# A 512-byte-per-partition copy as the first DMA on the ScalarE queue of a pooling kernel

## The chip, the core and the metric

The kernel runs on one core of a Trainium2 chip. Times are device microseconds (us); the time of a kernel is the median over its runs. Kernel before: 393.96 us, median of 3 runs (393.93 to 393.99). The core has compute engines with queues of their own (here VectorE and ScalarE do the arithmetic), SyncE, which here only issues DMAs, and 16 DMA engines that move data between the chip's memory (HBM) and the core's SBUF, which has 128 partitions. In the profile DVE is VectorE, ACT is ScalarE, SP is SyncE, and ACTq and SPq are the instruction queues from which ScalarE and SyncE issue DMAs.

## The reference

The kernel computes power-average pooling over windows of four along the last axis, with p = 2. `x` has 32 x 256 x 4096 float32 values, the result 32 x 256 x 1024.

```python
for i in range(out_length):                      # out_length = length // 4
    window = np.abs(x[:, :, 4*i:4*i + 4]) ** p    # p = 2
    result[:, :, i] = (np.mean(window, axis=-1)) ** (1.0 / p)
```

Each output is the square root of a quarter of the sum of four squares. 134.2 MB are read and 33.6 MB written, each once.

## The kernel before

The input is seen as one flat stream, cut into 20 loads of 128 rows, one row for each partition. A row has 13184 values (52,736 bytes, 6592 KB for the 128); load 3 has 13152 and load 19 has 11680. Loads are grouped into six blocks whose rows are contiguous in HBM: four of four loads, then loads 18, 16, 17, then load 19. One store writes the results of one block, so there are six stores.

Three tiles `xt` take the loads in turn. For each load i: ScalarE squares the tile in place (`square`, line 89), VectorE adds neighbours in two steps (`pairs`, line 95, then `fours`, line 99, to a quarter of the width), ScalarE takes the root with a scale of one quarter (`root`, line 102). The sums and roots of blocks 0 to 3 lie in `ot`, one slot for each load of the block; sums of loads 4, 8, 12 and 16 go first to PSUM (`st`), so that they need not wait for the store of the block before. The results of the last two blocks lie in the freed columns of an `xt` tile.

The order of the instructions on each engine is written out by hand (`tc.manual_schedule()`): each engine runs its own in program order, and semaphores make it wait for others.

- SyncE issues all 20 loads (line 83): three before the loop, then load i + 3 as soon as `fours` of load i is done, since it overwrites the same tile. It also issues the stores of blocks 3, 4 and 5 (line 86). These DMAs are queue q1.
- ScalarE issues the stores of blocks 0, 1 and 2 (line 86, called by `roots` for loads 3, 7 and 11), right after the block's last root. These are queue q10. The first is issued when load 3's results are ready.
- Before its first square ScalarE runs a root on a one-column tile `first`; the load of its function table stands ahead of it.
- VectorE's first instruction of its own is `pairs` of load 0.

For loads 18 and 19 VectorE squares part of the columns itself (line 155).

Of the kernel before, what the change touches and what calls it, by code (L numbers as in the profile page):

```python
# [1 line left out]

# [4 lines left out]


@with_exitstack
def kernel(  # L10
    ctx: ExitStack,
    tc: tile.TileContext,
    x: bass.AP,
    p: float,
    kernel_size: int,
    out: bass.AP,
):

    nc = tc.nc

    assert float(p) == 2.0, "kernel specialized for p == 2"
    k = int(kernel_size)  # L30
    assert k == 4, "kernel specialized for kernel_size == 4"

    P = nc.NUM_PARTITIONS
    fp32 = mybir.dt.float32
    Act = mybir.ActivationFunctionType
    add = mybir.AluOpType.add
    xf = x.rearrange("b c l -> (b c l)")
    of = out.rearrange("b c l -> (b c l)")
    total = xf.shape[0] // P

    W = 13184
    R = W // k
    X_SLOTS = 3
    NARROW = W - 32
    LAST = total - 18 * W - NARROW
    widths = [W] * 3 + [NARROW] + [W] * 15 + [LAST]
    n = len(widths)
    assert 0 < LAST <= W and LAST % 16 == 0


    blocks = [[0, 1, 2, 3], [4, 5, 6, 7], [8, 9, 10, 11], [12, 13, 14, 15], [18, 16, 17], [19]]
    block_of = {i: b for b, group in enumerate(blocks) for i in group}
    block_width = [sum(widths[i] for i in group) for group in blocks]

    x_pool = ctx.enter_context(tc.tile_pool(name="x_pool", bufs=1))
    o_pool = ctx.enter_context(tc.tile_pool(name="o_pool", bufs=1))
    s_pool = ctx.enter_context(tc.tile_pool(name="s_pool", bufs=1, space=bass.MemoryType.PSUM))
    x_tiles = [x_pool.tile([P, W], fp32, name=f"xt{j}") for j in range(X_SLOTS)]
    o_tile = o_pool.tile([P, 4 * R], fp32, name="ot")
    first = o_pool.tile([P, 1], fp32, name="first")  # L60
    s_tile = s_pool.tile([P, 4096], fp32, name="st")
    ctx.enter_context(tc.manual_schedule())

    def rows(flat, b, div):
        at = sum(block_width[:b]) * P // div
        return flat[at:at + block_width[b] * P // div].rearrange("(p w) -> p w", p=P)


    free = x_tiles[17 % X_SLOTS]
    place = {i: o_tile[:, i % 4 * R:i % 4 * R + widths[i] // k] for i in range(16)}  # L70
    place[18] = free[:, R:2 * R]
    place[19] = free[:, 0:LAST // k]
    place[16] = free[:, 2 * R:3 * R]
    place[17] = free[:, 3 * R:4 * R]
    held = [o_tile[:, 0:w // k] for w in block_width[:4]] + [free[:, R:4 * R], place[19]]

    xs, loads, stores, sums, squares = {}, {}, {}, {}, {}

    def load(i):
        b = block_of[i]  # L80
        at = sum(widths[j] for j in blocks[b][:blocks[b].index(i)])
        xs[i] = x_tiles[i % X_SLOTS][:, 0:widths[i]]
        loads[i] = nc.sync.dma_start(out=xs[i], in_=rows(xf, b, 1)[:, at:at + widths[i]])  # L83

    def store(b, queue):
        stores[b] = queue.dma_start(out=rows(of, b, k), in_=held[b])  # L86

    def square(v):
        return nc.scalar.activation(out=v, in_=v, func=Act.Square)  # L89

    def pairs(v):

        q = v.rearrange("p (n j) -> p n j", j=k)
        h = v[:, 0:v.shape[1] // 2].rearrange("p (n j) -> p n j", j=2)
        return nc.vector.tensor_tensor(out=h, in0=q[:, :, 0:2], in1=q[:, :, 2:4], op=add)  # L95

    def fours(o, v):
        h = v[:, 0:v.shape[1] // 2].rearrange("p (n j) -> p n j", j=2)
        return nc.vector.tensor_tensor(out=o, in0=h[:, :, 0], in1=h[:, :, 1], op=add)  # L99

    def root(o, s):
        return nc.scalar.activation(out=o, in_=s, func=Act.Sqrt, scale=1.0 / k)  # L102

    summed = {i: s_tile[:, 0:R] if i in (4, 8, 12, 16) else place[i] for i in range(n)}

    def roots(*group):
        if len(group) == 1:
            root(place[group[0]], summed[group[0]])
        else:
            v = o_tile[:, group[0] % 4 * R:(group[-1] % 4 + 1) * R]  # L110
            r = root(v, v)
            if group[0] in (5, 9):

                implied(r, stores[block_of[group[0]] - 1])
        if group[-1] in (3, 7, 11):
            store(block_of[group[-1]], nc.scalar)

    def implied(later, earlier):

        tc.declare_no_dep(later.ins, earlier.ins, reason="implied by the other waits")  # L120

    for i in range(X_SLOTS):
        load(i)


    ahead = {4: (3,), 8: (7,), 12: (11,)}
    behind = {3: [(0, 1, 2)], 7: [(5, 6), (4,)], 11: [(9, 10), (8,)], 14: [(12,)], 15: [(13, 14)], 16: [(15,)]}

    root(first[:, :], nc.const_aps.tensor(1.0, (P, 1), fp32))
    for i in range(17):  # L130
        if i in ahead:
            roots(*ahead[i])
        s = square(xs[i])
        squares[i] = s
        if i == 3:
            implied(s, squares[0])
        if i in (3, 7, 11):

            for earlier in sums[i - X_SLOTS]:
                implied(s, earlier)  # L140
        for group in behind.get(i, []):
            roots(*group)
        sums[i] = pairs(xs[i]), fours(summed[i], xs[i])
        if i + X_SLOTS < n:
            load(i + X_SLOTS)

    store(3, nc.sync)
    square(xs[17])
    pairs(xs[17])
    fours(summed[17], xs[17])  # L150
    later = {18: 4608, 19: 2000}

    def shared_square(i):
        v = xs[i][:, 0:later[i]]
        nc.vector.tensor_tensor(out=v, in0=v, in1=v, op=mybir.AluOpType.mult)  # L155
        square(xs[i][:, later[i]:widths[i]])

    def shared_pairs(i):
        implied(pairs(xs[i]), loads[i])

    shared_square(18)
    roots(16)
    roots(17)
    shared_pairs(18)
    fours(summed[18], xs[18])
    shared_square(19)
    roots(18)
    store(4, nc.sync)
    shared_pairs(19)
    fours(summed[19], xs[19])  # L170
    roots(19)
    store(5, nc.sync)


# [1 line left out]
_INS = ['x', 'p', 'kernel_size']  # L176
_OUTS = [((32, 256, 1024), 'float32')]

_NUMBERS = {'p': 2.0, 'kernel_size': 4}


# [26 lines left out]
```

## Time and profile before

| What | Value |
|---|---|
| time, median of 3 runs | 393.96 us (393.93 to 393.99) |
| span of the profiled execution, first to last instruction | 392.3 us |
| time of the runs outside such a span | 1.7 us (393.96 - 392.3) |
| ACT busy | 274.4 us (70%), 37 instructions |
| DVE busy | 218.2 us (56%), 42 instructions |
| DMA moved | 167.77 MB, mean 428 GB/s, 3744 packets |
| chain that ended last | DMA 43%, ACT 30%, DVE 23% |

The profile lists no time of its own for the profiled execution beside its span; the runs' times are those of the table. A line of the timeline has start, duration, engine, source line, operation and its tiles, and in brackets how long the engine was idle before it and what ended that. A line of a table by stretches has the stretch, its length, busy time and number of instructions of DVE, ACT and POOL, TensorE's clock, the mean busy share of the DMA engines and GB/s; a DMA packet is counted whole in the stretch in which it starts, so a short stretch can have a share above 1. A line of the DMA issues has tiles, issuing queue, number, KB each and the median us from issue to landing; a line of the DMA queues has packets, MB and the share of the 16 engines' span.

The 3744 packets are 26 DMAs of 128 rows and 16 semaphore writes each: one packet for a row, and 8 rows on each of the 16 engines.

### The profile page before, as it was taken

To read this page: it belongs to the slowest core of one execution; us is meant where nothing else is said; L and a number is where in the kernel's file an instruction comes from. 1 tells how busy PE (TensorE), PEld (TensorE's weight loads), DVE (VectorE), ACT (ScalarE), POOL (GpSimd) and SP (SyncE) were. 2 spreads that over 40 slices of the span, in tenths; PEclk is the share of its full clock that TensorE was granted. 3 is DMA by queue.
4 is the path that set the end of the run, shared out by engine and by line. 5 is a ranking of instruction groups with operands and counts; after the bars stand their busy time and mean duration, and the time that the engine had idled before them with its cause. 6 is when DMAs were issued, how large, how long until landed. Compare 5 with 4: busy or idle time off the path is not lost.

```text
span 392.3 us, 176 instructions
## 1 busy us (share of the span) xinstructions
DVE 218.2 (56%) x42; ACT 274.4 (70%) x37; POOL 0.2 (0%) x4
## 2 busy tenths in 40 slices
DVE  0009477580693274905942748069418485699970
ACT  1095695979950859799509597995098999969910
POOL 0000000000000000000000000000000000000000
DMA  8999999999999999999999999999999999999997
GB/s 344 430 430 430 430 440 435 452 457 366 430 430 430 430 430 430 430 441 446 452 446 441 436 430 436 430 430 430 430 430 430 430 430 430 430 453 415 430 413 342
DMA packets 3744, 167.77 MB, mean 428 GB/s; under 512 B 416, under 2 KB 416, under 8 KB 416
## 3 DMA queue, kind: packets, MB, share of 16 engines
q1 hardware_dynamic: 3312, 147.53, 87.4%
q10 hardware_dynamic: 432, 20.25, 11.9%
HBM read 134.22 MB, written 33.55 MB: 428 GB/s over the span
## 4 chain that ended last, share of the span: by engine, by line
DMA 43%; ACT 30%; DVE 23%; issue 0%; ACTq 0%; SPq 0%; DVEq 0%
DMA xt<-in_x_dram 43%; ACT xt L89 28%; DVE xt L95 14%; DVE ot L99 5%; DVE xt L99 3%; DVE xt L155 2%; ACT ot L102 2%; ACT xt L102 1%; ACTq L86 0%; SPq L83 0%; DVEq L95 0%
## 5 line engine op out<-in xcount | busy, mean ns | idle before, releaser
L89 ACT ACTIVATE xt<-xt 128x13184 f32<-128x13184 f32 (+3 forms) x20 | 216.7, 10847 | 92.3 <-DMA xt<-in_x_dram 91.0
L95 DVE TENSOR_TENSOR xt<-xt 128x6592 f32<-128x6592 f32 (+2 forms) x20 | 139.7, 6985 | 144.1 <-ACT xt L89 143.9
L99 DVE TENSOR_TENSOR ot<-xt 128x3296 f32<-128x3296 f32 (+1 forms) x13 | 46.7, 3592 | 17.9 <-DMA out_dram<-ot 17.6
L102 ACT ACTIVATE ot<-ot 128x6592 f32<-128x6592 f32 (+3 forms) x8 | 37.2, 4655 | 7.0 <-DVE ot L99 7.0
L102 ACT ACTIVATE xt<-xt 128x3296 f32<-128x3296 f32 (+1 forms) x3 | 8.5, 2836 | 8.8 <-DVE xt L99 8.8
L99 DVE TENSOR_TENSOR st<-xt 128x3296 f32<-128x3296 f32 x4 | 14.4, 3600 | 0.1
L99 DVE TENSOR_TENSOR xt<-xt 128x3296 f32<-128x3296 f32 (+1 forms) x3 | 10.4, 3461 | 0.1
L102 ACT ACTIVATE ot<-st 128x3296 f32<-128x3296 f32 x3 | 8.7, 2898 | 0.0
L155 DVE TENSOR_TENSOR xt<-xt 128x4608 f32<-128x4608 f32 (+1 forms) x2 | 7.2, 3593 | 0.0
L102 ACT ACTIVATE xt<-st 128x3296 f32<-128x3296 f32 x1 | 2.9, 2898 | 0.0
L102 ACT ACT_TABLE_LOAD x1 | 1.3, 1283 | 0.7 <-PEq L189 0.7
L102 ACT ACTIVATE first<-const-float32-1.0 128x1 f32<-128x1 f32 x1 | 0.2, 202 | 0.0
L189 POOL MEMSET const-bfloat16-1.0<- 128x1 bf16 x1 | 0.1, 101 | 0.0
L189 POOL MEMSET const-uint8-127<- 128x1 uint8 x1 | 0.1, 101 | 0.0
L189 POOL MEMSET const-float32-0.0<- 128x1 f32 x1 | 0.1, 98 | 0.2 <-issue 0.2
L189 POOL MEMSET const-float32-1.0<- 128x1 f32 x1 | 0.1, 98 | 0.0
## 6 DMA issues: line engine op xcount, KB each, us to landing
xt<-in_x_dram SPq DMA_DIRECT2D x18, 6592.0 KB, 29.8
out_dram<-ot ACTq DMA_DIRECT2D x2, 6592.0 KB, 35.1
out_dram<-ot SPq DMA_DIRECT2D x1, 6592.0 KB, 37.1
out_dram<-ot ACTq DMA_DIRECT2D x1, 6588.0 KB, 36.3
xt<-in_x_dram SPq DMA_DIRECT2D x1, 6576.0 KB, 24.7
xt<-in_x_dram SPq DMA_DIRECT2D x1, 5840.0 KB, 21.9
out_dram<-xt SPq DMA_DIRECT2D x1, 4944.0 KB, 16.1
out_dram<-xt SPq DMA_DIRECT2D x1, 1460.0 KB, 8.2
```

The lines of the kernel that those rows point to most:

```text
L89: return nc.scalar.activation(out=v, in_=v, func=Act.Square)
L95: return nc.vector.tensor_tensor(out=h, in0=q[:, :, 0:2], in1=q[:, :, 2:4], op=add)
L99: return nc.vector.tensor_tensor(out=o, in0=h[:, :, 0], in1=h[:, :, 1], op=add)
L102: return nc.scalar.activation(out=o, in_=s, func=Act.Sqrt, scale=1.0 / k)
L155: nc.vector.tensor_tensor(out=v, in0=v, in1=v, op=mybir.AluOpType.mult)
L189: nc = _bacc.Bacc("TRN2", target_bir_lowering=False, num_devices=1)
```

## The change

Two tiles of 128 columns, `zeros` and `spare`, are added in SBUF, behind the tiles that are there. Ahead of everything else VectorE sets `zeros` to 0. After the first three loads (which SyncE issues), ScalarE issues a DMA that copies `zeros` to `spare`, 512 bytes on each of 128 partitions, 64 KB in all. In ScalarE's program it stands ahead of the one-column root. It waits for the memset. Nothing reads `spare`.

```diff
     o_tile = o_pool.tile([P, 4 * R], fp32, name="ot")
     first = o_pool.tile([P, 1], fp32, name="first")
     s_tile = s_pool.tile([P, 4096], fp32, name="st")
+    zeros = o_pool.tile([P, 128], fp32, name="zeros")
+    spare = o_pool.tile([P, 128], fp32, name="spare")
     ctx.enter_context(tc.manual_schedule())
...
+    nc.vector.memset(zeros[:, :], 0.0)
     for i in range(X_SLOTS):
         load(i)
+    nc.scalar.dma_start(out=spare[:, :], in_=zeros[:, :])
```

## The prediction

> **What bounds the kernel now.** I read the page first: its slices, its DMA queues and its issues.
>
> ```profile
> DMA  8999999999999999999999999999999999999997
> q1 hardware_dynamic: 3312, 147.53, 87.4%
> q10 hardware_dynamic: 432, 20.25, 11.9%
> out_dram<-ot SPq DMA_DIRECT2D x1, 6592.0 KB, 37.1
> out_dram<-xt SPq DMA_DIRECT2D x1, 4944.0 KB, 16.1
> out_dram<-xt SPq DMA_DIRECT2D x1, 1460.0 KB, 8.2
> ```
>
> The 16 DMA engines work in every slice; the two queues' shares add to 99.3% of the span. q1 is SyncE's queue (20 loads, the last three stores), q10 ScalarE's (the first three stores). That this holds to the last microsecond is seen from the last stores: they are issued at 339.1, 371.8 and 383.1 us and land at 376.2, 387.9 and 391.3, so 4944 KB took 11.7 us and 1460 KB took 3.4, the rate of the loads (6592 KB in 15.57 us, 423 KB/us). ScalarE (70%) and VectorE (56%) wait. So time taken from the DMA engines' stream comes off the span, and time added to it goes on.
>
> Then the timeline, for the first square on each load's landing and the issues between.
>
> ```profile
> 0.73 1.28 ACT L102 ACT_TABLE_LOAD   x1 [0.73 <-PEq L189]
> 0.73 1.33 SPq L83 DMA_DIRECT2D xt<-in_x_dram  x3
> 2.02 0.20 ACT L102 ACTIVATE first<-const-float32-1.0 128x1 f32<-128x1 f32 x1
> 18.79 11.19 ACT L89 ACTIVATE xt<-xt 128x13184 f32<-128x13184 f32 x1 [16.56 <-DMA xt<-in_x_dram]
> ...
> 65.47 11.16 ACT L89 ACTIVATE xt<-xt 128x13152 f32<-128x13152 f32 x1 [4.34 <-DMA xt<-in_x_dram]
> ...
> 90.31 0.38 ACTq L86 DMA_DIRECT2D out_dram<-ot  x1
> ...
> 144.41 11.19 ACT L89 ACTIVATE xt<-xt 128x13184 f32<-128x13184 f32 x1 [4.36 <-DMA xt<-in_x_dram]
> ...
> 222.22 11.19 ACT L89 ACTIVATE xt<-xt 128x13184 f32<-128x13184 f32 x1 [4.38 <-DMA xt<-in_x_dram]
> ...
> 300.07 11.19 ACT L89 ACTIVATE xt<-xt 128x13184 f32<-128x13184 f32 x1 [1.58 <-DMA xt<-in_x_dram]
> ```
>
> Between these landings the engines move four loads and one store each time. 144.41 to 222.22 is 77.81 us, 222.22 to 300.07 is 77.85; 65.47 to 144.41, with the same bytes but 4 KB, is 78.94. So about 1.1 us are lost once, in the stretch that holds the first DMA on q10 (issued at 90.31). To find the place I asked for short stretches in which each of the 16 engines starts one row of a load or store. A packet is counted whole in the stretch where it starts, so the DMA share (the sixth number) times the width is the mean time of one packet.
>
> ```profile
> 1.70:2.60 0.90, 0.00 (x0) 0.51 (x2) 0.00 (x0) 1.00 2.96 938
> 4.30:4.90 0.60, 0.00 (x0) 0.00 (x0) 0.00 (x0) 1.00 3.25 1406
> 89.80:90.40 0.60, 0.00 (x0) 0.47 (x1) 0.00 (x0) 1.00 3.29 1406
> 91.80:92.40 0.60, 0.00 (x0) 0.60 (x1) 0.00 (x0) 1.00 4.82 1406
> 94.70:95.50 0.80, 0.00 (x0) 0.80 (x1) 0.00 (x0) 1.00 2.45 1054
> 170.55:171.30 0.75, 0.00 (x0) 0.75 (x1) 0.00 (x0) 1.00 2.60 1125
> 248.35:249.05 0.70, 0.00 (x0) 0.70 (x1) 0.00 (x0) 1.00 2.79 1205
> ```
>
> A row takes 1.95 us (4.30: 3.25 x 0.60). The rows started at 91.8 take 4.82 x 0.60 = 2.89 us, 0.94 more, on all engines at once; rows 1.3 us behind the second and third store's issues take 1.95. In the packet records those slow rows are still loads; the first store row starts at 94.8, after them. The only other slow rows are the very first, at 1.7 us: 2.96 x 0.90 = 2.66, 0.72 more. So both queues show one stall of 0.7 to 1.1 us, at their first DMA. SyncE's first store, at 339, shows none.
>
> **The change, part by part.** It removes nothing. It adds a memset of 128x128 f32 on VectorE, one DMA issue on ScalarE, and 64 KB of SBUF to SBUF traffic on q10, so that store 0 is no longer q10's first DMA.
>
> Memset: VectorE's adds take 7.03 us for 6592 columns, 1.07 ns each, so 0.14 us, up to 0.2 with the 0.1 us of a one-column memset as its fixed part. VectorE's first work comes at 30.01: free. Issue: 0.34 to 0.38 us on ScalarE (the three stores' rows), behind a wait for the memset, at about 0.95 if nothing is ahead of it. Queued behind it are the table load (1.28) and the one-column root (0.20), which then end near 2.9 instead of 2.2; the next, the square at 18.79, waits for load 0: free. SyncE's loads wait for none of this. No wait is added later, since nobody reads the spare tile, and the big tiles stay where they are.
>
> The copy's traffic: 128 rows over 16 engines, 8 packets of 512 B and a semaphore write each. By bytes alone 64 KB at 423 KB/us is 0.15 us. The packet records have 11,680 B at 0.438 us and 52,736 B at 1.947: a line through both gives 9 ns a packet and 0.037 ns a byte, 0.028 us for 512 B, so 8 x 0.028 = 0.22 us on each engine. I take 0.22, nearest in kind; ends 0.15 and 0.4 (double, for small packets that nothing here shows). It lies in a full stream, so it counts.
>
> The Trainium skill, in DMA: Bandwidth & Descriptors, section Bandwidth, measures 0.95 us for a lone 64 KB load and calls such transfers dominated by descriptors; by that the sum would be 0.73 us worse, about no change. I keep the row, since here the packets stand between those of loads.
>
> The stall at 91.8: it goes if it belongs to the queue's first DMA: -1.10 us by the landings (ends 0.94 by the rows, 1.13 by the longest difference). What replaces it at the start is not in the trace. Below, 0: the engines start the first rows at 1.74 to 2.49 and are slow there anyway; q10's first packets, issued 0.22 us after q1's, would arrive from 1.96 on, while those rows still wait (they end at 4.35 to 4.8, so data flow from 2.40 to 2.85). Above, 1.1, the whole stall in series. The nearest row is q1's own start, whose wait covers q10's arrival on most engines, so I take 0.
>
> Sum: -1.10 + 0.22 + 0 = -0.88 us. The profiled execution has a span of 392.3 us; the median of the runs, 393.96, has 1.7 more around it, which I leave. 393.96 - 0.88 = **393.1**. The case's own range: 392.9 (-1.13 with hardly any copy) to 393.4 (0.3 left at the start, 0.22 for the copy).
>
> **Rivals.** *Moved, not hidden.* The engines take the second queue's start in series with the first's: the stall of 0.7 to 1.1 us reappears in the second row, near 4.5 us. For it: if the issue stands behind the table load it leaves at 2.02 and reaches the engines after 3.0, when data already flow. Against: nothing but the order that I assume. -1.10 + 0.9 + 0.22 = about 394.0, from 393.4 to 394.2.
>
> *The stall is the first write to HBM, or to the output.* Then the copy touches neither, store 0 still stalls, and the copy costs 0.22: 394.2. For it: store 0 is also the first write. Against: the slow rows end before a store row starts, and later stores to other parts of the output have none.
>
> The Trainium skill, in DMA: Bandwidth & Descriptors, section Issuing engines are not separate DMA queues, says that a second issuing engine saves only issue time, which leaves no room for a queue's own start: it stands for this rival. The once-only loss of 1.1 us speaks against it.
>
> *Slower: two stalls for one.* Each kind of transfer, not each queue, is slow at first: the copy, the first from SBUF to SBUF, stalls the engines in rows near 4.5 us, and the store, the first from SBUF to HBM, does so again at 92. +0.94 + 0.22 = +1.2: 395.1. It decides from a new stall of 0.6 us on with the old one kept. For it: the two stalls seen are also the firsts of two directions. Against: the same as for the rival before.
>
> **How the numbers follow.** A measurement of this kernel tells about 0.2%, 0.79 us, from no change: faster ends at 393.17, slower begins at 394.75. Hidden 0.47, of which 0.42 beyond the bound and 0.05 within; moved 0.21 and first write 0.10, both within; two stalls 0.22, slower. The predicted time is that of the likeliest, 393.1. For 8 in 10 the range begins at 392.85, the full stall without copy, and reaches into the slower case, to 395.0; the hidden case alone is 392.9 to 393.4.
>
> **What would show it.** Right: no row near 92 above 2.0 us, 65.4 to 144.3 in 77.9 us instead of 78.9, and load 0's square no later than 19.1. Moved: the stretch at 92 clean, but rows near 4.5 at 2.7 or more and the first square near 19.9. First write: the rows at 92 still at 2.9. I am wrong if the first square moves by more than 0.4 us, or if the stall at 92 stays.

## The result

The changed kernel takes 394.52 us (median of 20 runs, 394.33 to 394.92), the kernel before, beside it, 394.01 (20 runs, 393.88 to 394.24): ratio 1.0014, interval 1.0008 to 1.0019. That is 0.5 us slower where 0.9 us faster was forecast. The time is in the stated range and within the 0.2%, but clearly off from no change, and to the other side.

Half of it is not in the span. Over its 20 runs the changed kernel's span is 392.50 us on average and 2.05 us lie outside it; in 33 runs of the kernel before, the span is 392.2 (median) and 1.80 lie outside.

The page of the changed kernel, its DMA lines:

```profile
DMA packets 3888, 167.84 MB, mean 427 GB/s; under 512 B 432, under 2 KB 560, under 8 KB 560
q1 hardware_dynamic: 3312, 147.53, 87.3%
q10 hardware_dynamic: 576, 20.31, 12.0%
```

144 packets more on q10, the copy's 128 rows and 16 semaphore writes. The engines are as full as before (99.3%). Its timeline:

```profile
0.82 0.17 DVE L124 MEMSET zeros<- 128x128 f32 x1 [0.82 <-PEq L193]
1.02 0.53 ACTq L127 DMA_DIRECT2D spare<-zeros  x1
1.58 1.28 ACT L104 ACT_TABLE_LOAD   x1 [1.58 <-DVE zeros L124]
2.87 0.20 ACT L104 ACTIVATE first<-const-float32-1.0 128x1 f32<-128x1 f32 x1
19.19 11.19 ACT L91 ACTIVATE xt<-xt 128x13184 f32<-128x13184 f32 x1 [16.11 <-DMA xt<-in_x_dram]
...
65.93 11.16 ACT L91 ACTIVATE xt<-xt 128x13152 f32<-128x13152 f32 x1 [4.35 <-DMA xt<-in_x_dram]
...
90.76 0.38 ACTq L88 DMA_DIRECT2D out_dram<-ot  x1
...
144.68 11.19 ACT L91 ACTIVATE xt<-xt 128x13184 f32<-128x13184 f32 x1 [4.37 <-DMA xt<-in_x_dram]
...
222.53 11.19 ACT L91 ACTIVATE xt<-xt 128x13184 f32<-128x13184 f32 x1 [4.40 <-DMA xt<-in_x_dram]
```

The first square is 0.40 us later than before (19.19 against 18.79). From 65.93 to 144.68 it is 78.75 us, and from there to 222.53 it is 77.85: the 0.9 us that store 0 costs are still there. The table by stretches shows where (the sixth number, the DMA share, times the width is the mean time of a packet when each engine starts one in the stretch):

```profile
4.30:5.00 0.70, 0.00 (x0) 0.00 (x0) 0.00 (x0) 1.00 2.83 1205
6.25:7.00 0.75, 0.00 (x0) 0.00 (x0) 0.00 (x0) 1.00 2.63 1136
92.00:92.70 0.70, 0.00 (x0) 0.70 (x1) 0.00 (x0) 1.00 3.75 1205
170.75:171.65 0.90, 0.00 (x0) 0.90 (x1) 0.00 (x0) 1.00 1.89 820
```

The second row of each engine, at 4.30, takes 2.83 x 0.70 = 1.98 us, and the third, at 6.25, among the copy's first packets (from 6.30), 2.63 x 0.75 = 1.97: the copy makes no stall of its own. The rows at 92 take 3.75 x 0.70 = 2.63 us. By the packet records (the start, length and size of every single packet, which the trace keeps) the next ones are slow as well; together they are 0.98 us over 1.95 a row (before: 0.96). The stall that the forecast wanted to lose is still in its old place, though ScalarE's queue had already been used.

### The profile page after: what moved, and what is told of

The parts are those of the page before. It is cut to its first block, busy times and chain, and to the rows that moved or that the text cites. A ratio compares the mean times of both kernels' runs of the same rounds, so it can differ in the third digit from the quotient of the medians.

```text
span 392.6 us, 178 instructions
## 1 busy us (share of the span) xinstructions
DVE 218.4 (56%) x43; ACT 274.4 (70%) x37; POOL 0.2 (0%) x4
## 4 chain that ended last, share of the span: by engine, by line
DMA 43%; ACT 30%; DVE 23%; issue 0%; ACTq 0%; SPq 0%; DVEq 0%
DMA xt<-in_x_dram 43%; ACT xt L91 28%; DVE xt L97 14%; DVE ot L101 5%; DVE xt L101 3%; DVE xt L159 2%; ACT ot L104 2%; ACT xt L104 1%; ACTq L88 0%; SPq L85 0%; DVEq L97 0%
```

## The experiments

### Which first write makes the stall at 92 us?

The early copy with another target: the output (by ScalarE's queue, then by SyncE's), and a tensor of its own in HBM. Then store 0 itself on SyncE's queue.

```diff
-    nc.scalar.dma_start(out=spare[:, :], in_=zeros[:, :])
+    nc.scalar.dma_start(out=rows(of, 0, k)[:, 0:128], in_=zeros[:, :])     # e1_warm_out
+    nc.sync.dma_start(out=rows(of, 0, k)[:, 0:128], in_=zeros[:, :])       # e2_warm_out_sync
+    nc.scalar.dma_start(out=nc.dram_tensor("scratch", (P, 128), fp32,
+                        kind="Internal").ap(), in_=zeros[:, :])            # e6_warm_scratch
```

> The early copy on the ScalarE queue goes from zeros to the first 512 bytes of each of block 0's rows in the output, which store 0 overwrites later, and not to a spare tile. Theory W (the stall at 92 us is the first write to HBM): no load row near 92 above 2.1 us; the stall comes with the early copy, as rows of 2.6 to 3.0 us that start between 4.3 and 8.5 us, and the first square starts near 20.0; 65.9 to 144.7 shrinks from 78.75 to about 77.9. Time about 394.2, or about 393.5 if the stall at the start overlaps the first loads' own wait. Rival S (the stall belongs to the first large store, when loads and stores first run side by side): rows at 92 stay at 2.7 to 2.9 us, time 394.5.

> As the run before, but SyncE issues the copy to the output, behind the first three loads in its own queue, so that its rows run behind load 2's, near 50 us, and ScalarE's queue is still first used by store 0. Theory W: the stall moves to about 48 to 52 us (rows of 2.6 us and more there), rows at 92 at 1.95; time 394.2. Rival Q (a stall for the first use of each queue, and another for something else): rows near 92 stay slow, since store 0 is the ScalarE queue's first DMA. Rival S: rows near 92 stay slow.

> As the first run, but the 64 KB go to a tensor of their own in HBM, which nothing reads, not to the output. Theory W in its wide form (any first write to HBM): as in the first run, the stall at 92 gone. Theory W in its narrow form (first touch of the output's addresses): a clean start, first square near 19.2, and rows at 92 at 2.7 to 2.9 us; time 394.5. Rival S: the same as the narrow form.

Measured: 394.60, 394.62 and 394.55 us against 394.02 (ratios 1.0015 [1.0007, 1.0024], 1.0015 [1.0006, 1.0024], 1.0014 [1.0005, 1.0023]), all like the changed kernel. The stretch at 92 of the first:

```profile
91.95:92.75 0.80, 0.00 (x0) 0.80 (x1) 0.00 (x0) 1.00 3.56 1055
```

3.56 x 0.80 = 2.85 us a row; the second has 3.55 in the same stretch. With the scratch tensor the excess is spread over three rows, 1.17 us in all by the packet records. So an earlier use of ScalarE's queue, an earlier write to HBM and an earlier write to the output, each of 512 bytes a row, all leave the stall in its place: "first DMA of a queue" falls, and "first write" falls for writes of this size.

For the fourth run the line in `roots` became

```diff
-            store(block_of[group[-1]], nc.scalar)
+            store(block_of[group[-1]], nc.sync if group[-1] == 3 else nc.scalar)
```

> The kernel before, with store 0 issued by SyncE and no early copy. Its rows then stand behind loads 5 and 6 in the same queue, and no load row of another queue runs beside them. Theory W: slow rows by about 0.9 us once, where store 0's first rows come up (near 110 to 115 us), and none at 92; the ScalarE queue's first DMA, store 1 near 172, shows none. Rival Q: slow rows near 172 us, with the first DMA of the ScalarE queue. Rival S: none before two queues run side by side, near 172. The time moves with the place of store 0 in the queue as well, by under 2 us, and is not judged.

394.68 us (runs from 394.08 to 398.75; ratio 1.0024 [1.0004, 1.0044]). No packet is slow at 92; the load rows just ahead of store 0's rows, which now stand behind load 6, are:

```profile
109.20:110.00 0.80, 0.80 (x1) 0.80 (x1) 0.00 (x0) 1.00 3.35 1055
```

3.35 x 0.80 = 2.68 us, 0.73 over a row. The store was issued at 90.43, 19 us earlier. So the stall goes with the store's first rows at the DMA engines, on either queue, and not with the issue. Around store 1, ScalarE's first DMA in this kernel, rows were slow by 0.14 us at 172 and by 0.32 at 185; that fits neither of the two theories fully.

### Is it the row's length, or store 0's own form?

Early stores to block 0's rows from the result tile, on ScalarE's queue: 8 KB of each row; 16 whole rows, one for each DMA engine; 26 KB of each row. Store 0 overwrites all of it.

```diff
+    nc.vector.memset(o_tile[:, 0:2048], 0.0)          # e10: all columns; e16: 0:2 * R
     for i in range(X_SLOTS):
         load(i)
+    nc.scalar.dma_start(out=rows(of, 0, k)[:, 0:2048], in_=o_tile[:, 0:2048])                    # e9_warm_1mb
+    nc.scalar.dma_start(out=rows(of, 0, k)[0:16, :], in_=o_tile[0:16, 0:block_width[0] // k])    # e10_full_rows
+    nc.scalar.dma_start(out=rows(of, 0, k)[:, 0:2 * R], in_=o_tile[:, 0:2 * R])                  # e16_half_rows
```

> An early store of 1 MB (VectorE zeros 2048 columns of the result tile, ScalarE's queue writes them to the head of block 0's rows in the output, 8 KB on each of 128 partitions; store 0 overwrites them). Its traffic costs 2.4 us, so the time is about 396.7 and isn't the point. Theory L (the stall belongs to the first store that writes at some length, not to the first write): rows of 2.6 us and more between 4 and 12 us, rows near 94 (92 and the shift) at 1.95. Theory R (the stall belongs to the first store with full rows of 52 KB beside full load rows, or to store 0's rows in themselves): the rows there stay at 2.6 to 2.9.

396.98 us (ratio 1.0072 [1.0056, 1.0087]). Rows of 8 KB, 64 KB through each engine, neither stall nor help. The rows ahead of store 0's, and those one turn earlier:

```profile
92.50:93.05 0.55, 0.00 (x0) 0.50 (x1) 0.00 (x0) 1.00 3.54 1534
94.45:95.00 0.55, 0.00 (x0) 0.55 (x1) 0.00 (x0) 1.00 5.17 1534
```

1.95 us, then 5.17 x 0.55 = 2.84.

> A look at one place. VectorE zeros the result tile (about 14 us), then ScalarE's queue writes 16 whole rows of block 0, 52,704 bytes each, one for each DMA engine, to the output, where store 0 overwrites them: 2 us of traffic some 75 us ahead of store 0. Theory R (the stall belongs to the first store of whole rows, wherever it comes): load rows of 2.6 us and more near 16 to 22 us, and rows near 94 at 1.95. Theory N (it belongs to store 0's place or form, not to being the first): rows near 94 stay at 2.6 to 2.9. Time near 396.5, not judged.

The early whole rows, all from 16 partitions, took 2 to 8 us each and the kernel 406.55 us (one run), so the start is a disturbance of its own. But the load rows ahead of store 0's are clean:

```profile
98.70:99.95 1.25, 0.00 (x0) 1.25 (x1) 0.00 (x0) 1.00 1.56 675
```

1.56 x 1.25 = 1.95 us. The half rows on all partitions (one run, 402.49 us) have no such disturbance:

> A look at one place. As the 1 MB store, with rows of 26 KB on all 128 partitions (VectorE zeros 6592 columns first, some 7 us; the store is 3.4 MB, 7.8 us of traffic; store 0 overwrites it). Theory R (the stall goes with the first long rows): load rows of 2.5 us and more near 10 to 14 us, ahead of the store's first rows, and the rows ahead of store 0, near 100 us, at 1.95. If only rows of 52 KB make it, or only 16 rows did, slow rows stay near 100. Time near 402, not judged.

```profile
8.20:8.85 0.65, 0.00 (x0) 0.65 (x1) 0.00 (x0) 1.00 3.07 1298
10.15:10.85 0.70, 0.00 (x0) 0.00 (x0) 0.00 (x0) 1.00 3.74 1205
98.35:99.10 0.75, 0.00 (x0) 0.63 (x1) 0.00 (x0) 1.00 2.60 1125
100.30:101.05 0.75, 0.00 (x0) 0.75 (x1) 0.00 (x0) 1.00 2.60 1125
```

At 10.15, ahead of the early store's first rows (12.9 us), a row takes 3.74 x 0.70 = 2.62 us; ahead of store 0 it takes 1.95 twice. Here the stall has moved: it belongs to the first store with long rows. The amount written does not decide: the early store of e10 put 52 KB through each engine and spared store 0 the stall, that of e9 put 64 KB through each and did not.

The other reading was that store 0's rows are special, since they alone are 52,704 bytes. For that load 7 was made the narrow one instead of load 3.

```diff
-    widths = [W] * 3 + [NARROW] + [W] * 15 + [LAST]
+    widths = [W] * 7 + [NARROW] + [W] * 11 + [LAST]
```

> The kernel before with load 7 made narrower instead of load 3, so that store 0's rows are 52,736 bytes like those of stores 1 and 2 were, and store 1's are 52,704 (not a multiple of 64). If the row form makes the stall, the rows at 92 are at 1.95 and slow rows stand near 171; time about 394.0. If being the first makes it, slow rows stay at 92 and none come at 171. Time 394.0 either way.

394.09 us against 394.00, ratio 1.0003 [0.9995, 1.0012]. Slow rows stay with store 0, spread over two turns, and store 1, now with the odd rows, has none:

```profile
93.80:95.30 1.50, 0.00 (x0) 1.50 (x1) 0.00 (x0) 1.00 1.79 563
170.35:171.25 0.90, 0.00 (x0) 0.90 (x1) 0.00 (x0) 1.00 2.16 938
```

1.79 x 1.50 = 2.69 us at 94, 2.16 x 0.90 = 1.94 at 170. Being first makes it, not the form.

Last, stores cut into rows of 13 KB, by one DMA for each load's results, for blocks 0 to 4 or for block 0 alone.

```diff
-        stores[b] = queue.dma_start(out=rows(of, b, k), in_=held[b])
+        dst, src, w = rows(of, b, k), held[b], block_width[b] // k
+        step = R if b in SPLIT else w          # e17: SPLIT = (0, 1, 2, 3, 4); e18: (0,)
+        stores[b] = [queue.dma_start(out=dst[:, c:min(c + step, w)], in_=src[:, c:min(c + step, w)])
+                     for c in range(0, w, step)]
```

> The kernel before, with the stores of blocks 0 to 4 cut into DMAs of one load's results each, rows of 13 KB in place of 52 KB. Theory R with a bound above 13 KB: no slow rows anywhere but at the start; the span then loses the 1.0 us of the stall and pays for 15 DMAs more (8 packets each at 4 to 9 ns of fixed time, 0.5 to 1.1 us): 393.5 to 394.1. With a bound under 13 KB: slow rows of 2.6 us near 92, 394.5 to 395.1. Stores take four times as many turns beside the loads, so they land later; if the sums wait for that, the time is longer by some us and isn't judged.

> The kernel before, with store 0 alone cut into four DMAs of 13 KB rows. Theory R with a bound above 13 KB: rows at 92 at 1.95, slow rows of 2.6 to 2.9 us near 171, ahead of store 1's first rows; time about 394.1 to 394.4. Bound under 13 KB: slow rows at 92, none at 171, 394.1 to 394.4.

Both are slower: 398.57 us (ratio 1.0074 [1.0037, 1.0112]) and 398.09 (1.0091 [1.0057, 1.0126]). But the times scatter: of the first kernel's ten runs four took 394.53 to 394.83 us, with a span only 0.1 to 0.4 us over the 392.3 before, and six took 398.48 to 399.31; the second's went from 396.29 to 399.84. The traces are of long ones, 399.14 and 399.84. In the second a short row (0.49 us) mostly takes its turn against a load row of 52 KB (1.95 us), so the store lands late, its last part 79.0 us after the issue, where the whole store took 36.3 before. VectorE's sums then wait 46.2 us for stores, against 17.6 before:

```profile
out_dram<-ot ACTq DMA_DIRECT2D x1, 1644.0 KB, 79.0
DVE ot L103 <- DMA out_dram<-ot: 46.2, 5, 10.4
```

What sets a run of the first kernel on one side or the other is not shown. In the second kernel three groups of load rows are slow:

```profile
95.05:95.50 0.45, 0.00 (x0) 0.45 (x1) 0.00 (x0) 1.00 5.65 1875
174.50:175.00 0.50, 0.00 (x0) 0.50 (x1) 0.00 (x0) 1.00 4.86 1688
178.75:179.85 1.10, 0.00 (x0) 1.10 (x1) 0.00 (x0) 1.00 2.89 767
```

The rows at 95 take 5.65 x 0.45 = 2.54 us, 0.6 too much; they run among store 0's short rows, which begin at 92.1. (In the first kernel the rows at 94.9 are 0.43 too slow.) The rows at 174.5, 0.47 too slow by the packet records, started before store 1 was issued at 176.17, so they are not its; they are the first of a load issued only at 173.22. The rows at 178.8, right ahead of store 1's first whole rows at 181.9, take 2.89 x 1.10 = 3.18 us, 1.23 too much. So neither bound that was expected holds: store 0 in rows of 13 KB makes a part of a stall, and the first store of whole rows makes a whole one all the same, where half rows (e16) had spared it that.

How the stall's size goes with the row is not shown beyond this: none at 8 KB, 0.4 and 0.6 us at 13 KB, 0.7 at 26 KB, and at 52 KB, over the traces of this case, from about 0.7 (e8) to 1.2 (e5), with 0.96 before the change.

### What the copy and the memset cost

```diff
     nc.vector.memset(zeros[:, :], 0.0)              # e7_memset_only: this alone
...
+    nc.scalar.dma_start(out=spare[:, :], in_=rows(xf, 0, 1)[:, 0:128])        # e8_read_in: this alone
```

> The changed kernel without the copy: the zeros tile and VectorE's memset alone. Theory M (the 0.25 us more outside the span comes with the memset, or with the larger program on VectorE): time minus span 2.05, span 392.2, time 394.25. Theory D (it comes with the added DMA): time minus span 1.80, time 394.0, no change.

> An early DMA of the same shape on ScalarE's queue without a memset: it reads 512 bytes of each of load 0's rows from HBM into the spare tile. Theory D: time minus span 2.05; theory M: 1.80. The span as in the changed kernel, 392.4 to 392.6. The stall at 92 us stays (2.7 to 2.9 us a row), since nothing is stored early.

The memset alone: 394.30 against 394.12 (ratio 1.0006 [0.9997, 1.0015]); span 392.29 against 392.32 on average, but 2.06 us outside. The DMA alone: 394.21 (1.0004 [0.9996, 1.0013]); span 392.46, 1.79 outside. By these two runs the memset costs about 0.27 us outside the span and nothing in it, and the early DMA costs only in it.

For the traffic the copy was issued four times. The first try had one target:

```diff
     nc.scalar.dma_start(out=spare[:, :], in_=zeros[:, :])
+    nc.scalar.dma_start(out=spare[:, :], in_=zeros[:, :])     # three times more
```

> The changed kernel with the copy issued four times, so 3 x 64 KB of small packets more. If the copy's traffic costs what its packets take (8 packets of about 23 ns on each engine, 0.18 us for 64 KB), three more add 0.55 us to the span: 393.05 against 392.5, time about 395.1. If the changed kernel's extra 0.25 us of span is instead a fixed price of an early DMA on ScalarE's queue, the time stays near 394.6. The 0.25 us outside the span: stays at 2.05 if it belongs to the memset or to the queue, grows toward 2.8 if it belongs to each DMA.

421.68 us, which says nothing of the traffic: each copy waits for the one before, since both write the same tile, and ScalarE waits with it. The timeline shows how long a 64 KB copy takes in this stream:

```profile
1.02 0.52 ACTq L127 DMA_DIRECT2D spare<-zeros  x1
21.04 0.47 ACTq L128 DMA_DIRECT2D spare<-zeros  x1
40.75 0.47 ACTq L129 DMA_DIRECT2D spare<-zeros  x1
50.77 0.47 ACTq L130 DMA_DIRECT2D spare<-zeros  x1
```

20 us, as long as no gap lets it through: each of its 8 packets on an engine stands behind a load row of 1.95 us.

The same trace bears on the prediction's other stall, the slow rows at 1.7 us. The DMA engines stand idle from 52 to 75 us, until the fourth load on q1, issued at 74.62; its first rows are slow too:

```profile
75.55:76.55 1.00, 1.00 (x1) 1.00 (x1) 0.00 (x0) 1.00 2.64 842
```

2.64 x 1.00 = 2.64 us, 0.70 over a row, where the very first rows had 0.72 before. So this stall comes again when loads start on idle engines, and is no matter of a queue's first DMA either.

With separate targets:

```diff
     nc.scalar.dma_start(out=spare[:, :], in_=zeros[:, :])
+    for j in range(1, 4):
+        nc.scalar.dma_start(out=o_tile[:, j * R:j * R + 128], in_=zeros[:, :])
```

> The changed kernel with four early copies to four separate places (the spare tile and the heads of three parts of the result tile), so that none waits for another, as the four copies to one place did. If a copy costs what its packets take (8 x 23 ns = 0.18 us on each engine), three more add 0.55 us: span 393.0 to 393.1, time 395.1. If the price of the early DMA is one of its start, span 392.5, time 394.6. Outside the span 2.05 as with one copy, since there is one memset.

394.67 us against 394.00 (1.0019 [1.0010, 1.0028]); the span is 392.93 against 392.21 on average, 0.71 us (before rounding) for four copies, 0.18 for one. That is what the packets say: 27 ns each, and the next load row starts 23 ns after the packet's start, 8 x 23 = 184 ns. But only 1.79 us were outside, with the memset in place, where 2.05 had been expected: "the memset costs 0.27" can't be the rule.

### The time outside the span

> The memset alone, without the copy, moved behind VectorE's sums of load 0 (near 40 us). If the 0.27 us more outside the span come with VectorE having early work, they go: time minus span 1.80, time 394.0. If they come with a memset instruction in VectorE's program, wherever it stands, 2.06, time 394.3.

Its edit moves the memset behind the sums of load 0. 394.32 against 394.00 (1.0009 [1.0000, 1.0018]), 2.07 outside: the place doesn't matter. Sorted by the number of VectorE's instructions in the trace (its semaphore instructions included) the runs fall in order, so two more were made, with three memsets of one column added to the changed kernel and to the kernel before:

```diff
+    for j in range(3):
+        nc.vector.memset(pad[:, j:j + 1], 0.0)
```

> The changed kernel with three more memsets of one column on VectorE, 57 VectorE instructions in the trace. Theory C (the time outside the span goes by the number of VectorE's instructions, in steps of four): 1.79 outside, time 394.25 to 394.35, 0.2 to 0.3 less than the changed kernel although it does more. Rival (the memset, or an early wait behind it): 2.05 or more, time 394.5 to 394.6.

> The kernel before with three memsets of one column on VectorE and no copy, 56 VectorE instructions. Theory C: the steps seen are 1.79 (53), 2.05 (54), 2.16 (55), so 56 gives 2.2 to 2.4 outside if the time grows up to a block of four, or about 1.6 if it falls ahead of 57; span 392.2 to 392.3. Rival (one early memset is enough, number without effect): 2.05, time 394.3.

| VectorE instructions | kernels | mean us outside the span |
|---|---|---|
| 53 | before; e4, e8, e11 | 1.78 to 1.80; 1.77, 1.79, 1.78 |
| 54 | changed; e1, e2, e5, e6, e7, e12 | 2.05; 2.04 to 2.08 |
| 55 | e9, e18; e10, e16 (one run each) | 2.18, 2.17; 2.15, 2.19 |
| 56 | e15 | 2.19 |
| 57 | e13, e14 | 1.79, 1.80 |
| 59 | e17 | 2.10 |

The changed kernel with three memsets more has 1.80 outside and takes 394.20 us against 394.07 (ratio 1.0005 [0.9996, 1.0014]): no longer measurably slower than the kernel before, with the copy still in it. The kernel before with the three has 2.19 and takes 394.39 (1.0008 [0.9999, 1.0016]). So the time outside the span goes with the count of VectorE's instructions, up from 53 to 56 and back at 57; neither the memset's work nor its place moves it. Nor does the size of the whole program: e8 and e7 both have 177 instructions in the trace, and 1.79 and 2.06 us outside. That the pattern comes back every four is not shown: 59, with 2.10, does not repeat the 2.17 of 55. What happens in that time isn't in the trace.

## Why the prediction was wrong

**What bounds the kernel** held: the DMA engines are full to the end, and what the copy puts in their stream came off at the end. The once-only loss of 1.1 us in the stretch of store 0 was read rightly, in place and size.

**The step that failed** is "it goes if it belongs to the queue's first DMA: -1.10 us". The term was 0. Two stalls, both at a queue's first DMA, were taken for one cause with two cases; the start of q1 was the only other case, and it is also the start of everything. In e5 its slow rows come again at q1's fourth load, after idle time, so neither stall was a queue's first DMA. The rival that the profile seemed to speak against, "the stall is the first write to HBM", was right that store 0 would stall and near in time (394.2), but its reason fell too (e1, e2, e6). What the runs show is the first store with long rows (e9, e10, e16, e11). "The slow rows end before a store row starts" was held against that rival and proves nothing: with rows of 26 and 52 KB, early or late, the stall hit mostly the load rows just ahead of the store's.

**The copy's traffic**, 0.22 us, was 0.18 (e13). The Trainium skill, in DMA: Bandwidth & Descriptors, section Bandwidth, has 0.95 us for a 64 KB load from HBM that another engine, GpSimd, issues, and calls transfers under 64 KB dominated by descriptors; no run here has such a load alone. In a full stream these runs show 0.18 of cost for the copy, and 20 us until it lands. The Trainium skill, on the same page, section Issuing engines are not separate DMA queues, says that DMAs of all issuing engines run interleaved on the same 16 DMA engines. The trace agrees, with the copy's packets of 27 ns between load rows of 1.95 us. The section does not speak of a queue's first use; here that of ScalarE's queue cost no stall (1.98 and 1.97 us a row).

**The start**, "I take 0", was nearly right for the wrong reason. The copy did not arrive while the first rows waited: its first packets run at 6.3 us, behind two load rows on each engine, and there was no stall to hide. In the profiled runs the first square is 0.4 us later; the spans' averages leave about 0.05 us beside the 0.18, no more than the averages of the kernel before differ among themselves (392.22 to 392.32).

**Memset and issue** (0.14 to 0.2 us, 0.34 to 0.38 us) were 0.17 and 0.53, both hidden as said; the table load and the one-column root behind the issue end at 3.07 (near 2.9 was said).

**"1.7 more around it, which I leave"** is the second term that failed: it was 1.79 in the kernel before and became 2.05, 0.26 us, half of the whole change (e7, e13, e14).

The sum by the runs: 0 for the stall, +0.18 for the copy, about +0.05 at the start, +0.26 outside the span: +0.49, against +0.51 measured.

**Open.** Why the first store with long rows stalls all engines once, and what length of row it takes; that the stall can be moved rests on one trace each of e10 and e16. Open are also e4's slow rows near store 1 (0.46 us in all), the two groups of times of e17, and what the core does in the time outside the span. No version beat the kernel before: moving the stall forward pays it elsewhere in the same full stream, and the two kernels with shorter store rows were slower.

## What to carry to other kernels

A loss that occurs once has as many explanations as things that happen there for the first time; before paying for a warm-up, change each of them alone (queue, direction, target, size), and make the trial as long as the real transfer: here rows of 512 bytes and of 8 KB left the stall where it was, and rows of 26 KB moved it. A small DMA in a full stream is cheap in traffic (0.18 us for 64 KB) but lands late (20 us), so nothing should wait for it. Differences of a quarter of a microsecond can come from the time around the span: compare span and time separately, and test with a few idle instructions before an explanation is built on them.

## What had not been expected of the hardware

- The time outside the span went with VectorE's instruction count: 1.79, 2.05, 2.17, 2.19 us for 53 to 56, and 1.79 again for 57.
- The first store with long rows slows all 16 DMA engines once: nothing seen at 8 KB rows, 0.7 us at 26 KB, 0.96 at 52 KB in the kernel before (0.7 to 1.2 in others); later stores on either queue show none in the kernel before.
- Loads that start on idle DMA engines have slow first rows, by 0.72 us at the kernel's start and by 0.70 again after a gap at 75 us (e5).
- 16 whole rows from 16 partitions only were slow, 2 to 8 us a row (e10), where rows spread over all partitions take 1.95.
